# Two transformer blocks on one core: expert choices made one head earlier, and four modulation halves moved from POOL to PE

## The chip, the cores and the metric

The kernel runs on one core of one Trainium2 chip. The metric is device time in microseconds (us): the time of one execution of the whole program. Names of engines: PE is TensorE (matmuls), DVE is VectorE, ACT is ScalarE, POOL is GpSimd, SP is SyncE, which here only issues DMAs. All data are float32.

## What is computed

One sequence of 256 tokens of width 1024 goes through two blocks. Every modulation row (shift, scale, gate) is a product of one conditioning vector with a 1024-wide matrix.

```python
def first_block(x, c, ...):
    mod = (silu(c) @ w_ada + b_ada)            # shift1, scale1, gate1, shift2, scale2, gate2
    h = rmsnorm(x, norm1_w) * (1.0 + scale1) + shift1
    proj = h @ w_in
    mix = concat([hgrn2_group(proj), short_conv_group(proj)]) @ w_out
    x = x + gate1 * mix
    h = rmsnorm(x, norm2_w) * (1.0 + scale2) + shift2
    x = x + gate2 * peer(h, ...)
    return rmsnorm(x, final_norm_w)

def peer(h, w_query, sub_keys, expert_u, expert_v):   # per block of 128 tokens
    q = (xb @ w_query).reshape(T, 8, 2, 128)
    s = einsum('thpk,hpnk->thpn', q, sub_keys)          # 2 x 128 scores a head
    top_s, top_i = top_k(s, 16)
    best_s, best_pos = top_k(all 256 sums of the two halves, 16)
    idx = the 16 chosen of 16384 experts;  gate = softmax(best_s)
    act = gelu(einsum('td,thkd->thk', xb, expert_u[idx]))
    return einsum('thk,thkd->td', gate * act, expert_v[idx])

def second_block(x, c, ...):                # NSA attention, then MoBA attention
    for i in range(2):
        shift, scale, gate = split(silu(c) @ ada_w[i] + ada_b[i], 3)
        h = rms_norm(x, norm_g[i]) * (1 + scale) + shift
        x = x + gate * (nsa_mixer(h) if i == 0 else moba_mixer(h))
```

## The kernel before

**Stages.** The program first makes the modulation halves of the first block, its projections, the recurrent mixer and the convolution (`phase_a`). Then comes PEER (`phase_b`): two halves `t` of 128 tokens with eight heads `h` each, 16 heads in a list `seq`. The second block (`phase_c`) is a generator that `phase_b` steps from the ninth head on, and that ends the program.

**A head of PEER.** `query(h)` multiplies the normalized tokens with 256 columns of the query weights on PE (the matmul helper is L242) and ACT copies the result. `scores(h)` multiplies it with the subkeys (L823) and ACT copies it into a tile `sc` (for `t` = 0; two buffers). `topk(t, h)` finds the 16 experts on DVE (L836 to L883): maxima, indices, a table of sums, and at the end two tiles `ix` of row numbers and a gate `gt`. It is a generator that yields four times, so that its pieces can stand between other work. `dots(t, h, k)` gathers row `k` of `expert_u` for all 128 tokens by an indirect DMA from POOL's queue (L899, 512 KB) and multiplies and sums it with the tokens on DVE (L910). After the sixteenth, ACT applies gelu. `weigh` multiplies with the gate. `combine(t, h, k)` gathers the row of `expert_v` (L899 again), ACT makes a diagonal of weights (L935), and PE adds the weighted rows into PSUM (L937). The gathers of the first heads share eight buffers `gb`; later the sixteen `w` buffers of the weights come in.

**The order in the loop.** In head `i` of `seq`, for `k` from 0 to 15, the loop issues a dot of head `i` and, from `k` = 3 on, a combine of head `i` − 1. `pick` is `topk` of head `i` + 1, one piece of which is issued behind the dot at certain `k` (`PICK`, in the first head from `k` = 10 on), the rest behind the sixteenth dot. `query(h + 2)` is issued ahead of a head of the first half, `scores(h + 2)` at `k` = 13. Ahead of the loop a block of raised priority does `mixed(0)` (residual, norm and transposed tokens of the first half), query, scores and `topk` of head 0 for `t` = 0, `rows(0)`, `mixed(1)`, and query and scores of head 0 for `t` = 1. The row `ada15` is made behind head 1.

**Weights.** `stream` loads the weights through SP's queue in the order in which they are listed, two ahead of their use. A weight is four tiles of 512 KB from a ring of sixteen buffers `w`. A tile is loaded when the last reader of its buffer is through.

**Modulation halves.** `ada(r, w)` makes one half (512 numbers) of a row on PE: eight matmuls (L416), a copy by ACT, four transposes (L425), a reduction and an addition by DVE into `colv`. Four halves of the second block are made differently. `tick` loads a quarter of the weight into `val` from POOL's queue (L149), multiplies it there by the conditioning vector (L159) and adds it up (L160, L162). `ada_sum` then sums over partitions by four matmuls of one column (L170) and adds on DVE (L172). The four are rows 20, 21 (first needed for `norm_T(0, ...)`, the norm of the second attention), 18 and 19. `step` calls `tick` now and then in the course of the second block, `ready` completes what is left.

**The attention of the second block.** `attention` runs eight heads in a row (`k` below counts them); each has scores (L1406, mask L1213), a maximum (L1216), an exponential on ACT (L1225), the scaling by the sums (L1227, L1232), transposes (L1244) and the product with the values (L1262). The generator's user puts other work between the heads: `ada17` at `k` = 1, the gates at 2, the first half of the output projection (`out_proj`, L1314) at 4 and 5, `ada22` and the next norm at 6, `ada23` at 7.

Of the kernel before, what the change touches and what calls it, by code (L numbers as in the profile page):

```python
# [28 lines left out]
CBEATS = 3  # L29
# [40 lines left out]
class Net:  # L70
    def __init__(self, ctx, tc, d, out):
        self.tc, self.nc, self.d, self.out = tc, tc.nc, d, out
        self.ctx = ctx
        self.cp = ctx.enter_context(Pool(tc, "cp"))
        self.ps = ctx.enter_context(tc.tile_pool(name="ps", bufs=1, space=PSUM))
        self.n = 0
        self.later = []
        self.pend, self.hooks = [], []
        self.wait = False
        self.turn = 0  # L80
        self.rests, self.ahead, self.loads, self.awbuf = [], [], [], []
        self.pc = self.am = None
# [21 lines left out]
    def step(self):  # L104
        self.turn += 1
        if self.awbuf:
            self.settle(self.turn)
            self.tick()
        due = []
        for x in self.later:  # L110
            x[0] -= 1
        due = [x for x in self.later if x[0] <= 0]
        self.later = [x for x in self.later if x[0] > 0]
        for _, fn in due:
            fn()
# [25 lines left out]

    def tick(self):

        nc = self.nc
        while self.loads and len(self.ahead) < len(self.awbuf):
            r, q = self.loads.pop(0)
            w = self.awbuf.pop(0)
            self.awbuf.append(w)
            nc.gpsimd.dma_start(w, self.ada_src(r)[q * 256:q * 256 + 256].rearrange("(k p) n -> p k n", p=P))  # L149
            self.ahead.append((r, q, w))  # L150
        if not self.ahead or (self.ahead[0][1] == 0 and len(self.rests) == 2):
            return
        r, q, w = self.ahead.pop(0)
        if q == 0:
            self.n += 1
            self.adas = self.pc2.tile([P, 512], F32, name=f"adas{self.n}", tag="adas", bufs=2)
        s = self.adas
        c = (0 if r < 12 else 8) + q * 2
        nc.gpsimd.tensor_tensor(w, w, self.ca[:, c:c + 2, None].to_broadcast([P, 2, 512]), op=ALU.mult)  # L159
        nc.gpsimd.tensor_tensor(s, s if q else w[:, 1, :], w[:, 0, :], op=ALU.add)  # L160
        if q:
            nc.gpsimd.tensor_tensor(s, s, w[:, 1, :], op=ALU.add)  # L162
        if q == 3:
            self.rests.append((self.turn + CBEATS, lambda: self.ada_sum(r, s)))

    def ada_sum(self, r, s):

        p = self.bank()
        for j in range(4):
            self.nc.tensor.matmul(p[:, j:j + 1], s[:, j * P:(j + 1) * P], self.one, start=True, stop=True)  # L170
        v, hf = divmod(r, 2)
        self.nc.vector.tensor_add(self.colv[:, v, hf * 4:hf * 4 + 4], p[:, 0:4], self.bt[:, r * 4:r * 4 + 4])  # L172

    def ready(self, n):

        while len(self.loads) + len(self.ahead) > n * 4:
            self.tick()
            if len(self.rests) == 2:
                self.settle()
        self.settle()  # L180

    def settle(self, i=None):

        while self.rests and (i is None or self.rests[0][0] <= i):
            self.rests.pop(0)[1]()
# [597 lines left out]
    def phase_b(self):  # L783
# [32 lines left out]
        def scores(h, ts=(0, 2)):  # L816
            if ts[0] == 0:
                sc[0, h] = bq.tile([P, 256], F32, name=f"sc{h}", tag="sc", bufs=2)
# [152 lines left out]
        with self.tc.high_priority():  # L971
# [4 lines left out]
            self.rows(0)  # L976
            self.mixed(1)
            query(0, (1, 2))
            scores(0, (1, 2))
# [5 lines left out]
        query(1)  # L985
        scores(1)
        for i, (t, h) in enumerate(seq):
            if t == 0 and h < 6:
                query(h + 2)
            pick = topk(*seq[i + 1]) if i < 15 else iter(())  # L990
            if i == 8:
                self.rows(1)
            for k in range(16):
# [6 lines left out]
                if (k in PICK) if i else k >= 10:  # L1000
# [4 lines left out]
                if t == 0 and h < 6 and k == 13:  # L1005
                    scores(h + 2)
            go(pick)
            if i == 14:
# [9 lines left out]
            if i == 1:  # L1018
# [306 lines left out]
    def phase_c(self, pool):  # L1325
# [7 lines left out]
        def w1_(hf):  # L1333
            def part(q):
# [9 lines left out]
             wt("ks2", W, 1536, False), wt("kw2", W, 2048, False), wt("q02", W, 0, False), w1_(0), w1_(1), wt("q1", W, 512), wt("z0", W, 2608), A(16), wt("z1", W, 3120), A(17)] +  # L1344
            [wt("wo0", d["nsa_w_out_2"][0], 0, False), wt("wo1", d["nsa_w_out_2"][0], 512, False), A(22), A(23),
# [129 lines left out]
        self.awbuf = [val[0].rearrange("p k n -> p (k n)").rearrange("p (a b) -> p a b", a=2)]  # L1475
        self.loads = [(r, q) for r in (20, 21, 18, 19) for q in range(4)]
        self.tick()
# [57 lines left out]
        self.awbuf.append(val[1].rearrange("p k n -> p (k n)").rearrange("p (a b) -> p a b", a=2))  # L1535
# [60 lines left out]
        for k in self.attention([(1, i) for i in range(8)], False, score, value, weigh, zT, oT, extra):  # L1596
# [8 lines left out]
            elif k == 2:  # L1605
                self.drain()
                self.z_close(zT, oT)
                gn = self.gate_rows(8, self.bp, "gn")
            elif k == 4:
# [3 lines left out]
            elif k == 5:  # L1613
                next(op)
            elif k == 6:
                self.drain()
                self.ready(2)
# [4 lines left out]
            elif k == 7:  # L1622
                self.ada(23, get("ada23"))
                self.ready(0)
                self.awbuf = []
# [98 lines left out]
```

## Time and profile before

| | |
|---|---|
| time, median of 3 runs | 1273.39 us (1272.66 to 1278.49) |
| the profiled execution | 1271.74 us, of which the span 1270.0 us |
| PE busy in the span | 1073.0 us (84%) |
| DVE busy | 818.5 us (64%) |
| POOL busy | 580.4 us (46%) |
| ACT busy | 436.6 us (34%) |
| TensorE's granted clock, mean | 0.959 of 2.4 GHz |
| read from HBM | 394.90 MB |

The span goes from the first instruction to the last; 1.74 us of the execution lie outside it. Times in the rows below count from the start of the span. A row of an order of time gives the start, the duration, the instruction and, in brackets, how long the engine had been idle and what ended that. A group of instructions gives count, busy time, mean duration and idle time ahead of it. The DMA share is the mean share of the core's 16 DMA engines that were at work. The first gather stands at 215.72 us and the last part begins at about 945 us, when the gathers are over.

### The profile page before, as it was taken

The page shows a single profiled execution, that of the slowest core. Times are in us where ns is not written, and L with a number is a line of the kernel's source. Part 1 is how long each engine was busy: PE and PEld are TensorE (multiplying, and loading weights), DVE is VectorE, ACT ScalarE, POOL GpSimd, SP SyncE. Part 2 cuts the span into 40 slices and gives each one's busy share as a digit, 9 for nine tenths or more (in the row PEclk, how much of TensorE's full clock was granted, in tenths as well). Part 3 has the DMA queues.
Part 4 walks back from the last instruction along what each step waited for, and adds up shares of the span by engine and source line. Part 5 has one row for each costly group of instructions (what it writes and reads, how often), then busy time and mean ns, then how long its engine had stood idle before and what let it go on. Part 6 is the DMA issues. An engine that isn't in the chain of part 4 may idle for free.

```text
span 1270.0 us, 14586 instructions
## 1 busy us (share of the span) xinstructions
PE 1073.0 (84%) x4484; PEld 608.2 (48%) x4484; DVE 818.5 (64%) x2124; ACT 436.6 (34%) x939; POOL 580.4 (46%) x607
## 2 busy tenths in 40 slices
PE   6799999889877777777597777889999978798988
PEld 1789678655322222332232223334444656356866
DVE  3667555765676668756876756658735776667674
ACT  2643454212222222222342112224333443155661
POOL 0000001365777777675777766676724566500000
PEclk9899999989999999899899989999999979899989
DMA  9789876789999999998999999999999649133410
GB/s 323 272 286 327 284 243 237 292 322 328 383 417 415 415 414 415 412 415 347 365 410 409 409 406 405 406 408 398 374 398 320 200 170 343 34 133 109 157 67 34
DMA packets 144305, 396.93 MB, mean 313 GB/s; under 512 B 15246, under 2 KB 21604, under 8 KB 144228
## 3 DMA queue, kind: packets, MB, share of 16 engines
q0 software_dynamic: 76032, 276.86, 55.5%
q1 hardware_dynamic: 67852, 119.03, 26.7%
q8 instruction: 36, 0.59, 0.2%
q14 instruction: 41, 0.34, 0.1%
q10 hardware_dynamic: 344, 0.11, 0.0%
HBM read 394.90 MB, written 1.05 MB: 312 GB/s over the span
## 4 chain that ended last, share of the span: by engine, by line
PE 46%; DMA 23%; DVE 14%; issue 8%; POOL 6%; ACT 4%; SPq 0%; POOLq 0%; ACTq 0%; DVEq 0%
DMA gb<-in_peer_u_dram,ix 13%; PE peer L937 13%; DMA gb<-in_peer_v_dram,ix 7%; POOL gb L899 6%; PE pa L242 6%; PE pa L244 5%; PE pa L246 4%; PE pa L245 4%; DVE gb L910 4%; PE pa L416 2%; DMA w<-in_w_ada_dram 2%; PE po L1262 1%; DVE e L1232 1%; DVE wl L194 1%; PE pa L1244 1%
## 5 line engine op out<-in xcount | busy, mean ns | idle before, releaser
L937 PE MATMUL peer<-gb,dg 128*128 128x512 f32 x1008 | 485.4, 618 | 123.0 <-DMA gb<-in_peer_v_dram,ix 67.9
L910 DVE SCALAR_TENSOR_TENSOR gb<-gb,h 128x1024 f32<-128x1024 f32 x256 | 309.8, 1216 | 189.8 <-DMA gb<-in_peer_u_dram,ix 171.4
L937 PEld LDWEIGHTS peer<-gb,dg 128*128 128x128 f32 x1008 | 183.1, 194 | 393.0 <-issue 264.9
L899 POOL DMA_INDIRECT gb<-in_peer_u_dram,ix x256 | 241.4, 943 | 153.9 <-issue 52.5
L899 POOL DMA_INDIRECT gb<-in_peer_v_dram,ix x256 | 242.4, 947 | 108.1 <-issue 50.8
L935 ACT ACTIVATE dg<-ident,wgt 128x128 f32<-128x128 f32 x252 | 98.2, 400 | 453.0 <-PE peer L937 377.7
L194 DVE TENSOR_TENSOR wl<-w,wh 128x1024 fp32r<-128x1024 f32 x76 | 96.5, 1284 | 25.6 <-ACT wh L193 18.6
L193 ACT CAST wh<-w 128x1024 fp32r<-128x1024 f32 x76 | 77.9, 1051 | 25.5 <-DMA w<-in_nsa_w_in_dram 7.1
L790 POOL IOTA iota<- 128x54 f32 x1 | 0.2, 188 | 168.1 <-DVE wl L194 168.1
L242 PE MATMUL pa<-w,val 128*128 128x512 f32 x144 | 66.8, 606 | 0.1
L242 PE MATMUL pa<-h2T,w 128*128 128x256 f32 (+1 forms) x288 | 63.6, 371 | 0.3 <-ACT h2T L770 0.2
L242 PEld LDWEIGHTS pa<-h2T,w 128*128 128x128 f32 x288 | 52.3, 197 | 12.8 <-issue 5.8
L416 PE MATMUL pa<-w,ca 128*32 128x512 f32 x320 | 48.4, 622 | 7.2 <-ACT ca L353 4.5
L159 POOL TENSOR_TENSOR val<-val,ca 128x1024 f32<-128x1024 f32 x16 | 32.3, 2019 | 45.5 <-DMA val<-in_ada_w_dram 45.5
L244 PE MATMUL pa<-h1H,wh 128*128 128x256 f32 x160 | 45.8, 287 | 4.6 <-ACT wh L193 4.6
L245 PE MATMUL pa<-h1L,wh 128*128 128x256 f32 x160 | 45.4, 284 | 0.0
L246 PE MATMUL pa<-h1H,wl 128*128 128x256 f32 x160 | 45.2, 285 | 0.0
L242 PEld LDWEIGHTS pa<-w,val 128*128 128x128 f32 x144 | 28.0, 197 | 34.5 <-issue 32.3
L1232 DVE TENSOR_SCALAR e<-e,su 128x128 f32<-128x128 f32 (+1 forms) x96 | 37.9, 458 | 0.6
L244 PEld LDWEIGHTS pa<-h1H,wh 128*128 128x128 f32 x160 | 30.9, 193 | 5.0 <-ACT wh L193 5.0
L1225 ACT ACTIVATE e<-pb,mx 128x256 f32<-128x256 f32 x48 | 22.1, 476 | 26.5 <-DVE mx L1220 21.6
L246 PEld LDWEIGHTS pa<-h1H,wl 128*128 128x128 f32 x160 | 31.0, 195 | 0.3 <-DVE wl L194 0.3
(426 smaller groups left out, 1684.6 us busy)
## 6 DMA issues: line engine op xcount, KB each, us to landing
w<-in_w_ada_dram SPq DMA_DIRECT2D x48, 512.0 KB, 5.0
w<-in_nsa_w_in_dram SPq DMA_DIRECT2D x44, 512.0 KB, 10.9
w<-in_ada_w_dram SPq DMA_DIRECT2D x32, 512.0 KB, 6.9
w<-in_w_in_dram SPq DMA_DIRECT2D x28, 512.0 KB, 9.2
w<-in_moba_w_in_dram SPq DMA_DIRECT2D x20, 512.0 KB, 4.7
w<-in_peer_w_query_dram SPq DMA_DIRECT2D x16, 512.0 KB, 8.0
val<-in_ada_w_dram POOLq DMA_DIRECT2D x16, 512.0 KB, 5.4
w<-in_w_out_dram SPq DMA_DIRECT2D x8, 512.0 KB, 6.4
```

Of the source, the lines that this page charges most:

```text
L193: nc.scalar.copy(flat(h), flat(w))
L194: (second or nc.vector).tensor_tensor(flat(l), flat(w), flat(h).bitcast(F32), op=ALU.subtract)
L242: nc.tensor.matmul(out, lhs[0], rhs[0], start=start, stop=stop, skip_group_check=True)
L244: nc.tensor.matmul(out, lhs[0], rhs[0], start=start, stop=False, skip_group_check=True)
L245: nc.tensor.matmul(out, lhs[0], rhs[1], start=False, stop=False, skip_group_check=True)
L246: nc.tensor.matmul(out, lhs[1], rhs[0], start=False, stop=stop, skip_group_check=True)
L416: nc.tensor.matmul(p[32 * g:32 * g + 32, :], self.ca[:, co + kk:co + kk + 1].to_broadcast([P, 32]), self.wk(w, kk, 0, 512)[0], start=(k == ...
L899: nc.gpsimd.indirect_dma_start(out=b, out_offset=None, in_=table, in_offset=bass.IndirectOffsetOnAxis(ap=ix[k // 8][:, k % 8:k % 8 + 1], a ...
L910: i = v.scalar_tensor_tensor(b, b, 1.0, self.h2, op0=ALU.mult, op1=ALU.mult, accum_out=a[:, k:k + 1])
L935: nc.scalar.activation(dg, self.ident, AF.Copy, scale=w)
L937: nc.tensor.matmul(acc[t][:, n * 512:(n + 1) * 512], dg, b[:, n * 512:(n + 1) * 512], start=(h == 0 and k == 0), stop=(h == 7 and k == 15))
L1232: v.tensor_scalar(e[:, u, s], e[:, u, s], su[:, u, s:s + 1], None, op0=ALU.mult)
```

## The change

Two things are changed.

Choices. `topk` of head 1 (for `t` = 0), with the query and scores that it needs, is put ahead of the first dots, between `rows(0)` and `mixed(1)`; the second half of the tokens of query and scores follows for both heads behind `mixed(1)`. In the loop every index is one further: `query(h + 3)`, `scores(h + 3)`, and `pick` is `topk` of head `i` + 2. `sc` has three buffers. `PICK` holds for the first head too. `ada15` is made behind head 0. The pool of the choices is closed one head earlier.

Modulation. `tick`, `ada_sum`, `ready` and `settle` are gone. The four halves are made by `ada`: rows 20 and 21 at `k` = 3, rows 18 and 19 at `k` = 5. Their weights stand in the stream, 20 and 21 behind 17, 18 and 19 behind the output weights and ahead of 22 and 23.

```diff
         def scores(h, ts=(0, 2)):
             if ts[0] == 0:
-                sc[0, h] = bq.tile([P, 256], F32, name=f"sc{h}", tag="sc", bufs=2)
+                sc[0, h] = bq.tile([P, 256], F32, name=f"sc{h}", tag="sc", bufs=3)
...
             go(topk(0, 0))
             self.rows(0)
+            query(1, (0, 1))
+            scores(1, (0, 1))
+            go(topk(0, 1))
             self.mixed(1)
-            query(0, (1, 2))
-            scores(0, (1, 2))
+            for h in range(2):
+                query(h, (1, 2))
+                scores(h, (1, 2))
...
-        query(1)
-        scores(1)
+        query(2)
+        scores(2)
         for i, (t, h) in enumerate(seq):
-            if t == 0 and h < 6:
-                query(h + 2)
-            pick = topk(*seq[i + 1]) if i < 15 else iter(())
+            if t == 0 and h < 5:
+                query(h + 3)
+            pick = topk(*seq[i + 2]) if i < 14 else iter(())
...
-                if (k in PICK) if i else k >= 10:
+                if k in PICK:
...
-                if t == 0 and h < 6 and k == 13:
-                    scores(h + 2)
+                if t == 0 and h < 5 and k == 13:
+                    scores(h + 3)
             go(pick)
-            if i == 14:
+            if i == 13:
...
-            if i == 1:
+            if i == 0:
                 self.ada(15, get("ada15"))
...
-             ... A(16), wt("z1", W, 3120), A(17)] +
-            [wt("wo0", d["nsa_w_out_2"][0], 0, False), wt("wo1", d["nsa_w_out_2"][0], 512, False), A(22), A(23),
+             ... A(16), wt("z1", W, 3120), A(17), A(20), A(21)] +
+            [wt("wo0", d["nsa_w_out_2"][0], 0, False), wt("wo1", d["nsa_w_out_2"][0], 512, False), A(18), A(19), A(22), A(23),
              wt("mk", M, 1024), wt("mq0", M, 0), ...
...
-        self.awbuf = [val[0].rearrange("p k n -> p (k n)").rearrange("p (a b) -> p a b", a=2)]
-        self.loads = [(r, q) for r in (20, 21, 18, 19) for q in range(4)]
-        self.tick()
...
+            elif k == 3:
+                self.ada(20, get("ada20"))
+                self.ada(21, get("ada21"))
             elif k == 4:
                 wo = [get("wo0"), get("wo1")]
                 op = self.out_proj((oT,), wo, 0, gn)
                 next(op)
             elif k == 5:
                 next(op)
+                self.ada(18, get("ada18"))
+                self.ada(19, get("ada19"))
             elif k == 6:
                 self.drain()
-                self.ready(2)
                 self.ada(22, get("ada22"))
...
             elif k == 7:
                 self.ada(23, get("ada23"))
-                self.ready(0)
-                self.awbuf = []
```

Where it moves instructions. DVE, ahead of the first dots of PEER. `ix` and `gt` are what `topk` of head 0 ends with, `tkm<-sc` is how a choice begins, `gb<-gb,h` is a dot. Line numbers of the kernel after are 50 lower than those before here. Before:

```order
L881 RECIPROCAL tkn_2042<-tkn_2042 128x1
L871 TENSOR_TENSOR tkc_292_2023<-tkc_292_2023,tkc_2013 128x432
L882 TENSOR_SCALAR gt_2044<-gt_2044,tkn_2042 128x16
L872 TENSOR_REDUCE tkx_2024<-tkc_292_2023 128x8
L873 CAST ix_2026<-tkx_2024 128x8
L910 SCALAR_TENSOR_TENSOR gb_2169,act_2168<-gb_2169,h_2048 128x1024
```

After, the same place:

```order
L832 TENSOR_SCALAR gt_2044<-gt_2044,tkn_2042 128x16
L822 TENSOR_REDUCE tkx_2024<-tkc_292_2023 128x8
L794 MAX_INDEX tki_2082<-tkm_2081,sc_2076 128x8
L823 CAST ix_2026<-tkx_2024 128x8
L795 MATCH_REPLACE tks_2083<-tkm_2081,sc_2076 128x128
L793 MAX tkm_2081<-sc_2076 128x8
L796 MAX tkm_2081<-tks_2083 128x8
L794 MAX_INDEX tki_2082<-tkm_2081,sc_2076 128x8
L797 MAX_INDEX tki_2082<-tkm_2081,tks_2083 128x8
L795 MATCH_REPLACE tks_2089<-tkm_2081,sc_2076 128x128
L799 TENSOR_SCALAR tkm_2081<-tki_2082 128x16
L796 MAX tkm_2081<-tks_2089 128x8
```

Before, the first dot follows on the last `ix` of head 0 and the choice of head 1 begins behind the eleventh dot; after, that choice (`tkm_2081`) begins within the end of head 0's, and goes on between the first dots.

PE, where the sixth head of the attention ends and `ada22` begins. `pb<-maskb` is the mask of the next scores, `pa<-w,ca` a matmul of `ada`, `pa<-ident,os` its transposes, `pa<-ident,e` the transposes of the attention. Line numbers after are 46 to 50 lower. Before:

```order
L1213 MATMUL pb_7369<-maskb,identb 128x2x128
L170 MATMUL pa_7390<-one,adas_7088 128x1 x4
L416 MATMUL pa_7404<-w_7247,ca 32x512
L416 MATMUL pa_7404<-w_7249,ca 32x512
L416 MATMUL pa_7404<-w_7251,ca 32x512
```

After:

```order
L1167 MATMUL pb_7406<-maskb,identb 128x2x128
L375 MATMUL pa_7427<-ident,os_7380 128x128 x4
L366 MATMUL pa_7443<-w_7336,ca 32x512
L366 MATMUL pa_7443<-w_7338,ca 32x512
L366 MATMUL pa_7443<-w_7340,ca 32x512
L1198 MATMUL pa_7475<-ident,e_7311 128x128 x3
L366 MATMUL pa_7443<-w_7342,ca 32x512
```

The sum over `adas` is gone, the last of the added halves' transposes (row 19) stand in its place, and the matmuls of row 22 have transposes of the attention between them. SP's queue has sixteen loads more, and POOL's listing ends, but for two fills of `xn`, with the last gather.

## Rows read from the trace of the kernel before

**Rows 1.** Stretches: us; busy of PE, PEld, DVE, ACT, POOL; clock; DMA share; GB/s.

```profile
207.00:219.00 12.00, 11.32 (x69) 10.02 (x70) 8.43 (x44) 5.75 (x15) 2.67 (x3) 1.00 0.41 139
245.00:250.00 5.00, 3.26 (x12) 2.77 (x13) 5.00 (x15) 2.42 (x4) 0.00 (x0) 0.78 0.04 16
250.00:255.00 5.00, 5.00 (x22) 4.27 (x22) 4.93 (x28) 1.90 (x4) 0.58 (x1) 0.88 0.02 5
```

**Rows 2.** POOL in order of time around the hole: start, us, instruction [idle before <-releaser].

```profile
238.19 0.94 POOL L899 DMA_INDIRECT gb<-in_peer_u_dram,ix  x1 [0.88 <-DVE gb L910]
254.42 1.05 POOL L899 DMA_INDIRECT gb<-in_peer_u_dram,ix  x1 [15.29 <-DVE ix L873]
```

**Rows 3.** DVE in order of time: first dot, first choice row, last dot.

```profile
220.19 1.22 DVE L910 SCALAR_TENSOR_TENSOR gb<-gb,h 128x1024 f32<-128x1024 f32 x1 [3.30 <-DMA gb<-in_peer_u_dram,ix]
...
242.19 0.29 DVE L843 MAX8 tkm<-sc 128x8 f32<-128x128 f32 x1
...
249.38 1.22 DVE L910 SCALAR_TENSOR_TENSOR gb<-gb,h 128x1024 f32<-128x1024 f32 x1
```

**Rows 4.** PE in order of time, from the queries to the first combines.

```profile
208.80 4.71 PE L242 MATMUL pa<-h2T,w 128*128 128x128 f32 x32
...
214.53 7.07 PE L242 MATMUL pa<-h2T,w 128*128 128x256 f32 x32
...
240.96 1.92 PE L416 MATMUL pa<-w,ca 128*32 128x512 f32 x16
246.74 0.66 PE L425 MATMUL pa<-ident,os 128*128 128x128 f32 x4 [3.86 <-ACT os L420]
...
266.03 3.75 PE L937 MATMUL peer<-gb,dg 128*128 128x512 f32 x4 [4.27 <-DMA gb<-in_peer_v_dram,ix]
...
271.92 1.88 PE L937 MATMUL peer<-gb,dg 128*128 128x512 f32 x4
273.63 1.46 PE L242 MATMUL pa<-h2T,w 128*128 128x256 f32 x6
274.93 1.88 PE L937 MATMUL peer<-gb,dg 128*128 128x512 f32 x4
```

**Rows 5.** Groups by line, 955 to 1100 us, POOL: xcount | busy, mean ns | idle.

```profile
L159 POOL TENSOR_TENSOR val<-val,ca 128x1024 f32<-128x1024 f32 x16 | 32.3, 2019 | 45.5 <-DMA val<-in_ada_w_dram 45.5
```

**Rows 6.** Groups by line, 1030 to 1100 us, DVE.

```profile
L1232 DVE TENSOR_SCALAR e<-e,su 128x256 f32<-128x256 f32 x20 | 19.4, 1021 | 0.1
```

**Rows 7.** Groups by line, 1180 to 1250 us, DVE.

```profile
L1232 DVE TENSOR_SCALAR e<-e,su 128x256 f32<-128x256 f32 x16 | 4.5, 348 | 0.1
```

**Rows 8.** Waits of PE, 955 to 1100 us: waited for, total, times, longest.

```profile
PE po L1262 <- DVE os L1314: 8.3, 1, 8.3
PE pb L1406 <- ACT e L1225: 6.8, 1, 6.8
PE pa L1244 <- DVE e L1232: 3.3, 3, 1.5
PE pa L1174 <- DVE kd L1169: 2.4, 1, 2.4
```

**Rows 9.** DVE in order of time, the second run of scalings.

```profile
1091.37 6.01 DVE L1232 TENSOR_SCALAR e<-e,su 128x256 f32<-128x256 f32 x4
```

**Rows 10.** Stretches of the last part, columns as in rows 1.

```profile
1100.00:1110.00 10.00, 10.00 (x25) 4.43 (x24) 3.05 (x9) 1.93 (x8) 0.00 (x0) 0.77 0.00 0
1100.00:1130.00 30.00, 30.00 (x191) 16.51 (x190) 18.95 (x52) 12.88 (x35) 0.00 (x0) 0.92 0.20 71
```

**Rows 11.** PE in order of time, the same sixteen matmuls at two clocks.

```profile
1067.56 1.09 PE L1262 MATMUL po<-eT,V 128*64 128x128 f32 x16
...
1098.04 1.98 PE L1262 MATMUL po<-eT,V 128*64 128x128 f32 x16 [8.31 <-DVE os L1314]
```

**Rows 12.** SP's queue in order of time.

```profile
1055.64 7.86 SPq L129 DMA_DIRECT2D w<-in_ada_w_dram  x8
```

**Rows 13.** Issues of 1035 to 1130 us: xcount, KB, us to landing.

```profile
w<-in_ada_w_dram SPq DMA_DIRECT2D x9, 512.0 KB, 10.4
```

More of the change, by code (lines that the diff above doesn't have):

```diff
@@ L28 @@
 IDLE = 8
-CBEATS = 3
 SIDE = (1, 5, 9, 13)
@@ L80, in __init__ @@
         self.turn = 0
-        self.rests, self.ahead, self.loads, self.awbuf = [], [], [], []
         self.pc = self.am = None
@@ L105, in step @@
         self.turn += 1
-        if self.awbuf:
-            self.settle(self.turn)
-            self.tick()
         due = []
@@ L140, in half_row @@
         return self.tmp([P, 512], tag="xn" if self.am else "os")
[L142 to L185, printed above, removed]
     def split(self, w, second=None):
@@ L1343, in phase_c @@
             [wt("q1a", W, 512, False), wt("ks", W, 1536, False), wt("kw", W, 2048, False), wt("q0", W, 0, False), wt("kc", W, 1024, False),
-             wt("ks2", W, 1536, False), wt("kw2", W, 2048, False), wt("q02", W, 0, False), w1_(0), w1_(1), wt("q1", W, 512), wt("z0", W, 2608), A(16), wt("z1", W, 3120), A(17)] +
-            [wt("wo0", d["nsa_w_out_2"][0], 0, False), wt("wo1", d["nsa_w_out_2"][0], 512, False), A(22), A(23),
+             wt("ks2", W, 1536, False), wt("kw2", W, 2048, False), wt("q02", W, 0, False), w1_(0), w1_(1), wt("q1", W, 512), wt("z0", W, 2608), A(16), wt("z1", W, 3120), A(17), A(20), A(21)] +
+            [wt("wo0", d["nsa_w_out_2"][0], 0, False), wt("wo1", d["nsa_w_out_2"][0], 512, False), A(18), A(19), A(22), A(23),
              wt("mk", M, 1024), wt("mq0", M, 0), wt("mq1", M, 512), wt("mz0", M, 1536), wt("mz1", M, 2048),
@@ L1474, in phase_c @@
             self.split_T(val[0], hT, kk, 0)
-        self.awbuf = [val[0].rearrange("p k n -> p (k n)").rearrange("p (a b) -> p a b", a=2)]
-        self.loads = [(r, q) for r in (20, 21, 18, 19) for q in range(4)]
-        self.tick()
         yield
@@ L1534, in phase_c @@
             self.split_T(val[1], hT, kk, 1)
-        self.awbuf.append(val[1].rearrange("p k n -> p (k n)").rearrange("p (a b) -> p a b", a=2))
         w = get("q1")
```

## The prediction

> **What bounds the kernel now.** The page first, for PE's share of the span, the largest. It is an average over stages, so the two places of the change are read by themselves: by tables of stretches, then engine by engine in order of time.
>
> The head of PEER. The DMA engines are busy 4% and 2% of the time in the two slices from 245 to 255 us [rows 1]. That hole is POOL's: the sixteenth gather of head 0 issues at 238.19, the next starts at 254.42, after 15.29 us of waiting for `ix`, which `topk` of head 1 writes [rows 2]. DVE starts that `topk` only at 242.19, after eleven dots of head 0, and goes on with it between and behind the other five, the last of which starts at 249.38 [rows 3]. PE is then without work: the first weighting of rows of v starts at 266.03, after 4.27 us of waiting for its gather [rows 4].
>
> The last part. From 955 to 1100 us POOL multiplies and adds for the four modulation halves [rows 5]. In 1030 to 1100 DVE's 128x256 scaling at L1232 takes 1021 ns on average; in 1180 to 1250, with POOL silent, 348 [rows 6, 7]. PE waits for such a scaling, for an exponential behind slowed DVE work, for `kd`, and once 8.3 us for L1314 [rows 8], which stands on DVE behind two runs of four scalings, the second of 6.01 us [rows 9]. After such a pause TensorE's granted clock is a mixture of its two levels, 2.4 and 1.2 GHz (0.77 over ten busy us, [rows 10]), and sixteen L1262 matmuls take 1.98 us instead of 1.09 [rows 11].
>
> **The head, part by part.** `topk` of head 1 is issued ahead of the dots of head 0, and `topk` of head 2 between them. In DVE's listing the pieces of head 1 stand in front of and between the first dots, where DVE has idle time: the first dot starts at 220.19 after 3.30 us of waiting for its rows [rows 3]. So it is free from 216.9, and then has sixteen dots of 1.22 us and two choices of 8.4 (head 0's, all that DVE does in the first slice of [rows 1]): 216.9 + 19.5 + 16.8 = 253.2 without a wait. I take 254.5 for the end of head 0's last dot, instead of 250.6. Against that, head 1's rows are known by an estimated 235, and its u gathers can follow the sixteenth of head 0 as fast as dots free buffers (eight in this stage). By 254.4 I count eight gathers of it, some 10 us of transfer. The v rows of head 0 then lie ready, and the weighting waits only for gelu and `weigh`, an estimated 4.5 us behind the last dot: first combine at 259 instead of 266, a gain of 7.
>
> Two things take back from it. `query` of head 1 is made in two halves of tokens, each at 4.71 (head 0's second half) instead of 7.07 at once [rows 4], 2.3 us of PE, which has room there. And more of the queries is left when combining begins: from 271.92 on a v gather's matmuls (1.71 us) alternate with six query matmuls (1.30) [rows 4], 3.0 us where POOL's issue of a u and a v gather would take 2.5 (two of 0.94 and 0.31). About 5 us more of queries, at a loss of 0.5 for each 1.30, is 2 us. **Head: 7 − 2 = 5 us.** Bounds: 0, if the pace behind the hole is PE's anyway; 10, the hole's two slices in full (4.8 + 4.9). I take 5, as the wait of 15.29 is the row nearest and PE's alternation keeps it from being had in full.
>
> Behind it, up to the last heads, the gathers, dots and matmuls are the same, but for choices that stand one head earlier: nothing, and the gain passes on. `ada` of row 15 moved from the second to the first head, the third `sc` buffer and three memsets moved on POOL lie under the gathers; without that cover they are 1.92 + 0.66 us of PE [rows 4] at most.
>
> **The last part.** Removed on POOL: 16 multiplications (2.0 us each, [rows 5]), 28 additions, 16 loads. DVE gets its undisturbed times. Of PE's waits [rows 8] the 8.3 goes in full: eight scalings at 1021 − 348 ns are 5.4, the second run alone gives 4.6, the small operations between them are slowed too, and what is left of DVE's work lies under PE's own. The 3.3 goes. Of the 6.8 I take 2, of `kd` 2: the work ahead of them is slowed in part only. That is 15.6. Clock: 0.77 over ten busy us is 2.3 us lost [rows 10], and about as much after the two other long pauses; with one of these left, 5. **Relief 20**, next late is PE itself.
>
> Added on PE: four halves of 1.92 and 0.66 [rows 4], 10.3, less four sums of four short matmuls, 0.5 each by the transposes' row: **8 us**, all on PE's path. Their four ACT copies and DVE reductions lie under it. The 16 loads of 512 KB go from POOL's queue to SP's, the bytes are the same.
>
> New waits. Each weight is four buffers of a ring of sixteen that SP's queue fills in order. Rows 18 and 19 are loaded when PE has used 20 and 21; 22 and 23 when it has used 18 and 19; moba's k when it has used 22. Before, 22 and 23 were issued from 1055.64, in 7.86 us [rows 12], long before use. Now 22 must come between the fifth and the sixth head of the attention: four issues of about 1 us and their transfer, an estimated 7 us, about as long as one head. PE takes its instructions in order, so a late load holds the heads behind it. I take 2 us for all of it; bounds 0 and 12 (the median landing of 10.4, [rows 13], and 2 of low clock). **Last part: 20 − 8 − 2 = 10 us**, bounds 0 and 17.
>
> **Sum.** 5 + 10 = 15 off the profiled execution of 1271.74, which lies 1.65 below the runs' median of 1273.39: **1258** by the median. Bounds 0 and 27 off, 1246 to 1273.
>
> One row speaks against the head: next to DVE's choice the gather at 254.42 took 1.05 us, against 0.94 at 238.19 [rows 2]. At 0.11 more, sixteen gathers lose 1.8 us, which they have. The Trainium skill, "SBUF — State Buffer", section "SBUF: two separate sides", says more: while DVE runs an operation that takes both ports, POOL is locked out of the pair that they share and cannot write the descriptors of its own DMAs. By that rule gathers would stand still for a choice; that is rival 4.
>
> **Rivals.**
> 1. The head gains nothing. Either the pace behind the hole is PE's, 3.0 us for a pair of gathers [rows 4], and what comes earlier waits for queries; or the change doesn't do what it says, since eight buffers, freed by dots that now stand behind two choices, hold head 1's gathers as `ix` did. Against it: PE idles 4.27 before the first combine. Only the last part counts: 1273.4 − 10 = 1263. Chance 0.17.
> 2. POOL's relief is not PE's: DVE and ACT set the pace of the attention's heads, and the halves are pure addition. Against it: from 1100 on, with POOL silent, PE is busy 30.00 of 30 us [rows 10]. Relief 10 − 8 − 2, head 3: 1270. Chance 0.17.
> 3. Slower, by the ring: each of the loads of 18, 19, 22 and 23 is waited for on PE with its whole landing time (10.4, [rows 13]) and 2 of low clock. That is 4 × 12 = 48 in place of the 2: 1304. It decides from 24 us of such waits on, two of the four, where the time passes 1279.8. Against it: a pair issues together, so that the second is hidden by the first. Chance 0.09.
> 4. POOL is held by DVE's choices: head 1's gathers come later by one choice (8.4) than forecast, head −3 instead of +5: 1266. The 1.05 against 0.94 speaks against it. Chance 0.07.
>
> **How the numbers follow.** Forecast 0.50, 1258, own range 1250 to 1266. A measurement of this kernel can tell about 0.5% (6.4 us) from no change: faster ends at 1267.0, slower starts at 1279.8. Faster: 0.48 of the forecast, 0.15 of rival 1, 0.05 of rival 2, 0.04 of rival 4: 0.72. Same: 0.02, 0.02, 0.11, 0.03 and 0.01 of rival 3: 0.19. Slower: 0.08 of rival 3 and 0.01 of rival 2: 0.09. The range goes from 1245, the best case of the sum, to 1272, past rival 2.
>
> **What would show it.** Right: DMA engines busy over 0.7 of 245 to 255, no wait of POOL for `ix` over 5 us, the first combine near 259; L1232 near 350 ns throughout, no 8.3 us wait on PE. Wrong: PE waiting at L416 for `w` loads by over 2 us at rows 18 or 22 (rival 3); gathers above 1.1 us beside the choices (rival 4); the first combine early but pairs of gathers 3 us apart for longer than before (rival 1); PE still waiting for DVE in the attention's heads without POOL (rival 2).

## The result and the profile after

The kernel after takes 1249.61 us (median of 6 runs, 1246.89 to 1253.74), the kernel before 1273.62 (6 runs beside it). The ratio is 0.983, 95% interval 0.980 to 0.986: faster by 24 us in the medians, by 18 to 25 us by the interval. Its profiled execution takes 1246.89 us, the shortest of the six. The page of the kernel after, part 1 and the chain of work that ended last, and that chain before:

```profile
PE 1077.0 (86%) x4564; PEld 610.7 (49%) x4564; DVE 783.0 (63%) x2128; ACT 438.9 (35%) x944; POOL 494.2 (40%) x547
...
PE 59%; DMA 19%; DVE 7%; issue 6%; POOL 4%; ACT 4%; ACTq 0%; POOLq 0%; DVEq 0%
```

```profile
PE 46%; DMA 23%; DVE 14%; issue 8%; POOL 6%; ACT 4%; SPq 0%; POOLq 0%; ACTq 0%; DVEq 0%
```

POOL has 86 us less, DVE 36 us less although it has four instructions more, PE 4 us more. PE's share of the chain has grown from 46% to 59%, at the cost of DVE's and DMA's. To say where the time went I cut both traces at three marks: the start of the first gather, the first combine on PE, and the end of the last combine.

| us | before | after | difference |
|---|---|---|---|
| start to first gather | 215.7 | 213.3 | −2.4 |
| first gather to first combine | 50.3 | 43.7 | −6.6 |
| first gather to last combine (PEER) | 732.8 | 724.9 | −7.9 |
| last combine to the end | 321.5 | 306.9 | −14.6 |
| span | 1270.0 | 1245.1 | −24.9 |

The first line is no part of the change: other traces of both kernels start gathering between 215 and 218 us. The marks in the rows, before (L937) and after (L887): the last combines, from a window that begins at 925 us:

```profile
924.72 23.77 PE L937 MATMUL peer<-gb,dg 128*128 128x512 f32 x55
```

```profile
924.69 13.47 PE L887 MATMUL peer<-gb,dg 128*128 128x512 f32 x31
```

The head of PEER. Stretches after, columns as in [rows 1], where the slices from 245 to 255 had a DMA share of 0.04 and 0.02:

```profile
240.00:245.00 5.00, 5.00 (x24) 4.19 (x23) 5.00 (x21) 0.00 (x0) 1.89 (x3) 1.00 1.03 419
245.00:250.00 5.00, 3.56 (x29) 1.78 (x29) 4.65 (x21) 2.25 (x7) 2.80 (x3) 1.00 1.02 409
250.00:255.00 5.00, 5.00 (x26) 4.43 (x25) 5.00 (x15) 1.37 (x2) 1.06 (x1) 1.00 0.54 193
255.00:260.00 5.00, 5.00 (x18) 3.08 (x17) 5.00 (x20) 1.98 (x5) 3.64 (x4) 1.00 0.82 272
```

The hole is filled but for half a slice. POOL after, in order of time: the first gather of head 1, and the two longest waits among its gathers, which stand where 15.29 us stood [rows 2]:

```profile
236.01 0.94 POOL L849 DMA_INDIRECT gb<-in_peer_u_dram,ix  x1 [0.31 <-issue]
...
242.34 0.94 POOL L849 DMA_INDIRECT gb<-in_peer_u_dram,ix  x1 [4.15 <-DVE tki L797]
...
252.68 1.06 POOL L849 DMA_INDIRECT gb<-in_peer_u_dram,ix  x1 [3.89 <-DVE gb L860]
```

Head 1's gathers follow head 0's without a pause. What they wait for then is a free buffer, that is DVE, which has the pieces of a choice between the dots that free them. The row at 242.34 names a tile of the choice (`tki`), but it starts 0.27 us behind the end of head 0's eleventh dot (242.07), as that at 252.68 starts 0.28 behind the end of the sixteenth.

The last part. DVE's scaling (L1232 before, L1186 after) in 1000 to 1080 us, and PE's waits from 940 to 1080 us (waited for, total, times, longest). In [rows 6] and [rows 8] there stood 1021 ns and waits of 8.3, 6.8, 3.3 and 2.4:

```profile
L1186 DVE TENSOR_SCALAR e<-e,su 128x256 f32<-128x256 f32 x24 | 7.1, 349 | 0.2
```

```profile
PE pa L1525 <- DVE xn L1515: 2.4, 1, 2.4
PE pb L1360 <- ACT e L1179: 1.8, 1, 1.8
PE pa L1128 <- ACT os L1077: 0.8, 1, 0.8
```

Of these the 2.4 for `xn` is new: before, PE waited 0.2 us for it.

The halves that PE now makes (L366 and their transposes), in order of time:

```profile
1052.04 3.64 PE L366 MATMUL pa<-w,ca 128*32 128x512 f32 x32
1055.61 0.66 PE L375 MATMUL pa<-ident,os 128*128 128x128 f32 x4
...
1066.72 0.60 PE L375 MATMUL pa<-ident,os 128*128 128x128 f32 x4
...
1077.82 3.64 PE L366 MATMUL pa<-w,ca 128*32 128x512 f32 x32
...
1086.15 1.10 PE L366 MATMUL pa<-w,ca 128*32 128x512 f32 x6
```

The rows at 1052.04 and 1077.82 are rows 20, 21 and 18, 19, that at 1086.15 is the begin of row 22. None has idle time ahead of it: none of these matmuls waited for its weights. SP's queue after issued the loads of rows 18, 19, 22 and 23 in one stretch of 29.79 us instead of 7.86 [rows 12]:

```profile
1053.97 29.79 SPq L124 DMA_DIRECT2D w<-in_ada_w_dram  x16
```

### The profile page after: what moved, and what is told of

It is laid out like the page before. It is cut to its first block, busy times and chain, and to the rows that moved or that the text cites. A ratio compares the mean times of both kernels' runs of the same rounds, so it can differ in the third digit from the quotient of the medians.

```text
span 1245.1 us, 14741 instructions
## 1 busy us (share of the span) xinstructions
PE 1077.0 (86%) x4564; PEld 610.7 (49%) x4564; DVE 783.0 (63%) x2128; ACT 438.9 (35%) x944; POOL 494.2 (40%) x547
## 4 chain that ended last, share of the span: by engine, by line
PE 59%; DMA 19%; DVE 7%; issue 6%; POOL 4%; ACT 4%; ACTq 0%; POOLq 0%; DVEq 0%
PE peer L887 17%; PE pa L192 10%; DMA gb<-in_peer_v_dram,ix 9%; DMA gb<-in_peer_u_dram,ix 9%; PE pa L194 5%; PE pa L196 5%; PE pa L195 5%; POOL gb L849 4%; PE pa L366 3%; DVE gb L860 3%; PE po L1216 2%; PE pa L1198 1%; ACT dg L885 1%; PE pa L522 1%; PE pb L1360 1%
## 5 line engine op out<-in xcount | busy, mean ns | idle before, releaser
L887 PE MATMUL peer<-gb,dg 128*128 128x512 f32 x1008 | 486.7, 621 | 110.8 <-DMA gb<-in_peer_v_dram,ix 67.9
L887 PEld LDWEIGHTS peer<-gb,dg 128*128 128x128 f32 x1008 | 185.0, 195 | 380.2 <-issue 273.3
L144 DVE TENSOR_TENSOR wl<-w,wh 128x1024 fp32r<-128x1024 f32 x76 | 91.5, 1220 | 19.7 <-ACT wh L143 14.2
L366 PE MATMUL pa<-w,ca 128*32 128x512 f32 x384 | 57.4, 625 | 7.0 <-ACT ca L303 4.6
L377 DVE TENSOR_REDUCE adac<-pa 128x4 f32<-128x16 f32 x24 | 4.1, 171 | 48.1 <-PE pa L375 47.9
L195 PEld LDWEIGHTS pa<-h1L,wh 128*128 128x128 f32 x160 | 31.2, 195 | 0.0
```

Source lines behind the costliest of these rows:

```text
L144: (second or nc.vector).tensor_tensor(flat(l), flat(w), flat(h).bitcast(F32), op=ALU.subtract)
L195: nc.tensor.matmul(out, lhs[0], rhs[1], start=False, stop=False, skip_group_check=True)
L366: nc.tensor.matmul(p[32 * g:32 * g + 32, :], self.ca[:, co + kk:co + kk + 1].to_broadcast([P, 32]), self.wk(w, kk, 0, 512)[0], start=(k == ...
L887: nc.tensor.matmul(acc[t][:, n * 512:(n + 1) * 512], dg, b[:, n * 512:(n + 1) * 512], start=(h == 0 and k == 0), stop=(h == 7 and k == 15))
```

## The experiments

In the tables below PEER is first gather to last combine, and the rest is last combine to the end. The chip of the first pair of traces is not on record. The first four runs below share one chip; where a later run was on another this is said. The measure is always the kernel before, timed beside it on the same chip.

### Each part alone

The choices alone, on the kernel before. The edit is the choice part of the diff, of which two pieces are shown, with the modulation left on POOL:

```diff
             self.rows(0)
+            query(1, (0, 1))
+            scores(1, (0, 1))
+            go(topk(0, 1))
             self.mixed(1)
...
-            pick = topk(*seq[i + 1]) if i < 15 else iter(())
+            pick = topk(*seq[i + 2]) if i < 14 else iter(())
```

> The kernel before with the choices alone made earlier; the four modulation halves stay on POOL. Theory (the two parts add): the part of the span between the first gather and the last combine shortened by 7.9 us in the trace after, and nothing of that hangs on the halves: 8 us below before, ratio 0.994 (0.992 to 0.996). The first combine comes 6 to 7 us nearer to the first gather. Rival (the head gains nothing, the last part alone counts): the hole in the DMA is filled, but the last combine ends where it did, ratio 0.998 to 1.002.

Measured: 1266.53 us (10 runs), ratio 0.994 (0.989 to 0.998). In the trace PEER takes 723.1 us, the rest 322.0.

The halves alone, on the kernel after, with the choice part put back (two pieces shown):

```diff
-            query(1, (0, 1))
-            scores(1, (0, 1))
-            go(topk(0, 1))
             self.mixed(1)
...
-            pick = topk(*seq[i + 2]) if i < 14 else iter(())
+            pick = topk(*seq[i + 1]) if i < 15 else iter(())
```

> The kernel after with the choices as before; only the halves are moved to PE. Theory: from the last combine on, the trace after is 14.6 to 16 us shorter, so 15 us below before, ratio 0.988 (0.985 to 0.991); with the run of the choices alone the two gains sum to that of the whole change. Rival (the relief of DVE is mostly not on PE's path, and the whole change gains in PEER): ratio above 0.993.

Measured: 1258.91 us (4 runs), ratio 0.987 (0.982 to 0.992). PEER 731.7, the rest 307.9. So the parts add: one works in PEER and leaves the rest alone, the other the other way round, and 0.994 times 0.987 is 0.981. The rival of the second run is out by its interval; that of the first, which the interval touches at 0.998, by the trace, where the last combine ends 9.7 us earlier. A wait of PE for a weight stands in this trace, in PE's waits from 940 to 1110 us; the traces of four later runs have one too, of 0.3 to 1.0 us, those of the kernel after none:

```profile
PE pa L366 <- DMA w<-in_ada_w_dram: 0.8, 1, 0.8
```

### What in the last part was slow: POOL's arithmetic

```diff
-        nc.gpsimd.tensor_tensor(w, w, self.ca[:, c:c + 2, None].to_broadcast([P, 2, 512]), op=ALU.mult)
-        nc.gpsimd.tensor_tensor(s, s if q else w[:, 1, :], w[:, 0, :], op=ALU.add)
-        if q:
-            nc.gpsimd.tensor_tensor(s, s, w[:, 1, :], op=ALU.add)
+        nc.gpsimd.tensor_tensor(s[:, 0:4] if q else s, w[:, 0, 0:4] if q else w[:, 0, :],
+                                self.ca[:, c:c + 1].to_broadcast([P, 4 if q else 512]), op=ALU.mult)
+        nc.gpsimd.tensor_tensor(s[:, 0:4], s[:, 0:4], w[:, 1, 0:4], op=ALU.add)
```

> The kernel before with POOL's arithmetic on the four halves cut down: the 16 multiplications work on 4 columns of 1024 (the first of each half on 512), the additions on 4; the loads on POOL's queue, the sums on PE and all waits between them stay, so the four modulation halves are not what they should be. Theory (DVE and POOL hold each other up in the last part): L1232 falls from 1021 to about 350 ns, PE's waits of 8.3 and 3.3 us go, and as no work is added on PE the gain is larger than by the halves on PE, 20 to 23 us below before, ratio 0.982 to 0.985. Rival (the loads on POOL's queue, the sums or the places where the kernel waits for the halves cost the time): ratio 0.995 to 1.0, L1232 still above 700 ns.

Measured: 1251.51 us (4 runs), ratio 0.982 (0.977 to 0.987). PEER 732.7 as before, the rest 302.0. DVE's scaling (L1230 in this kernel) in 1000 to 1080 us, and PE's waits from 940 to 1110:

```profile
L1230 DVE TENSOR_SCALAR e<-e,su 128x256 f32<-128x256 f32 x20 | 5.8, 344 | 0.1
```

```profile
PE pb L1404 <- ACT e L1223: 4.8, 1, 4.8
PE pa L1172 <- DVE kd L1167: 1.0, 1, 1.0
PE cmp L1545 <- DVE kcT L1526: 0.9, 1, 0.9
PE pa L1573 <- DVE xn L1563: 0.2, 1, 0.2
```

The sixteen loads still go through POOL's queue, the sums and all waits between them are there, and POOL still runs 32 operations, 28 of them of 0.31 to 0.34 us, four of 1.2. The other long ones are gone, and with them the 1021 ns, the 8.3 and the 3.3 us [rows 6, 8]. So it is the long operations of POOL that held DVE up, and not its loads or the places at which the kernel waits for the halves. Two rows of the kernel before, DVE and POOL in order of time, show how:

```profile
1090.25 1.08 DVE L1415 TENSOR_TENSOR su<-su,gate 128x4 f32<-128x4 f32 x1
```

```profile
1090.06 1.26 POOL L160 TENSOR_TENSOR adas<-adas,val 128x512 f32<-128x512 f32 x1
```

DVE's operation, which takes 0.15 us on average in the trace after (L1369), starts within POOL's and ends with it, at 1091.33 and 1091.32. The Trainium skill, "SBUF — State Buffer", section "SBUF: two separate sides", has this as an exclusive lock on a port pair that the two engines share, held for a whole instruction. These two rows fit that; a test of the ports themselves is not among the runs. The rest is 19.5 us shorter than before: that is the relief without a price. The halves on PE, at 307.9, cost 5.9 us of it.

### One choice ahead or two

The choice of head 1 stays ahead of the first dots, but in the loop the choice is one head ahead, as before; nothing is chosen during head 0.

```diff
-        query(2)
-        scores(2)
         for i, (t, h) in enumerate(seq):
-            if t == 0 and h < 5:
-                query(h + 3)
-            pick = topk(*seq[i + 2]) if i < 14 else iter(())
+            if t == 0 and h < 6:
+                query(h + 2)
+            pick = topk(*seq[i + 1]) if 0 < i < 15 else iter(())
...
```

> The kernel after, but in the loop the choice is one head ahead, as before: only head 1 is chosen ahead of the first dots, and during head 0 nothing is chosen. Theory (the hole is that head 1's choice comes late, no more): the hole stays filled, DVE has one choice of 8.4 us less among head 0's dots, so head 0's last dot and the first combine come up to 5 us earlier than after: 1244 to 1250, ratio 0.977 to 0.982. Rival (two heads ahead are needed, else the hole comes one head later): 1255 to 1258, ratio 0.986 to 0.989, with POOL waiting for ix by 5 us or more at the begin of head 2's gathers.

Measured: 1248.28 us (4 runs), ratio 0.980 (0.975 to 0.984). PEER 720.5, the rest 307.6. Stretches of this kernel, columns as in [rows 1]:

```profile
245.00:250.00 5.00, 5.00 (x25) 4.40 (x24) 4.91 (x12) 0.54 (x2) 3.57 (x5) 1.00 1.03 418
250.00:255.00 5.00, 4.27 (x24) 3.56 (x23) 4.97 (x17) 2.02 (x6) 3.21 (x4) 1.00 1.03 419
```

The hole is filled without a remainder. Two heads ahead are not needed: no later hole appears, and the trace of PEER is 4 us shorter than that of the kernel after. The two intervals overlap, so that as a time this lead is not shown.

### Does PE's query work take the gain back?

A table of when the gathers of u of a head begin, in us from the first gather, read from POOL in order of time (head 8 is the first of the second half of tokens):

| first gather of u of head | 1 | 2 | 3 | 5 | 8 | 15 | last combine ends |
|---|---|---|---|---|---|---|---|
| before | 38.7 | 87.0 | 131.7 | 212.2 | 334.2 | 651.3 | 732.8 |
| after | 22.7 | 75.3 | 122.4 | 203.0 | 326.0 | 641.2 | 724.9 |
| after, third trace | 22.2 | 73.2 | 120.4 | 201.2 | 323.8 | 639.1 | 724.2 |
| head 1 only | 22.7 | 74.4 | 122.5 | 202.1 | 325.0 | 641.0 | 720.5 |
| half query (below), again | 22.9 | 74.6 | 114.4 | 194.5 | 317.7 | 632.5 | 719.0 |

Two rows of the kernel after from which such numbers come, head 0's first gather and head 3's:

```profile
213.29 1.25 POOL L849 DMA_INDIRECT gb<-in_peer_u_dram,ix  x1 [40.92 <-ACT h2T L720]
...
335.71 0.94 POOL L849 DMA_INDIRECT gb<-in_peer_u_dram,ix  x1 [0.30 <-issue]
```

Head 1 begins 16.0 us earlier than before, head 2 11.7, head 3 9.3, and from there on it stays at 8 to 10. To see whether PE's queries eat the 7 us, half of the query matmuls of heads 3 to 7 was left out:

```diff
+                kd = KD // 2 if h > 2 else KD
-                for k in range(KD):
+                for k in range(kd):
...
```

> The kernel after, with half of the query matmuls of heads 3 to 7 left out (four of eight blocks of the inner dimension), so that the choices of these heads are others; 5 times 3.5 us of PE's work is gone. Theory (behind the hole PE's queries between the combines set the pace, 3.0 us for a pair of gathers instead of 2.5): 5 to 10 us below the kernel after, ratio 0.973 to 0.979. Rival (the gathers' bytes set it): within 1.5 us of the kernel after, ratio 0.980 to 0.985.

Measured: 1330.19 us (10 runs), ratio 0.994 (0.990 to 0.999). The kernel after, run beside it on the same chip, had the same:

> The kernel after, unchanged, as the measure for the three that run beside it: 1247 to 1252 us, ratio 0.980 to 0.985.

Measured: 1330.49 us (12 runs, 1321 to 1338), ratio 0.996 (0.992 to 0.999). Both were on another chip, on which the kernel before takes 1339.47. The trace after has there 808.4 us of PEER and 308.1 of the rest: the gathers are slow, 365 GB/s from 400 to 600 us, against 399 in the third trace after. Stretches of the two, columns as in [rows 1], the slow chip first:

```profile
400.00:600.00 200.00, 133.86 (x252) 52.81 (x250) 108.61 (x308) 33.97 (x79) 130.95 (x139) 0.82 0.96 365
```

```profile
400.00:600.00 200.00, 149.75 (x311) 55.81 (x309) 133.72 (x372) 52.38 (x117) 145.26 (x170) 0.95 1.00 399
```

On that chip the question could not be decided, and the gain is less than half. So the kernels were run once more beside the kernel before and the kernel after:

> The kernel before, unchanged, for a trace beside the three others. From first gather to last combine 733 us and 321 to 323 us behind it where the gathers run as fast as in its first trace; where they run as slowly as in the four runs ahead of this one (792 to 808 us from first gather to last combine), over 800 us, and the part behind the last combine still 321 to 323: that part hangs on no gather.

Measured: 1275.31 us (a single run), PEER 732.5, the rest 322.9, on a third chip, with gathers as fast as in the first traces.

> The kernel after, unchanged, as the measure for the two below. Behind the last combine 306 to 309 us, 14 below before wherever it runs. From first gather to last combine 8 us below before if the gathers run as in the first traces (ratio 0.980 to 0.985); where they are slow, one theory (the hole of the DMA is filled, so its bytes are won at any pace) says 8 us again, ratio 0.982 to 0.985, the other (at the slower pace other waits take the gain) 0 to 3, ratio 0.987 to 0.990.

Measured: 1251.76 us (6 runs), ratio 0.984 (0.980 to 0.987), PEER 724.2, the rest 308.1: 8.3 and 14.8 us less than the kernel before beside it, as in the first pair of traces.

> The kernel after with half of the query matmuls of heads 3 to 7 left out, run again (the choices of these heads are others). Theory as it stands by the traces so far (PEER follows the first combine; PE's queries between the combines take nothing back): first gather to last combine within 2.5 us of the kernel after, ratio within 0.002 of its. Rival (PE's queries set the pace up to 325 us): 5 to 10 us shorter.

Measured: 1245.71 us (6 runs), ratio 0.978 (0.974 to 0.982), PEER 719.0. My theory at that moment, that PE takes nothing back, fell: the time is 6 us below that of the kernel after. Stretches of the kernel after (third trace) and, below it, with half the queries:

```profile
280.00:300.00 20.00, 19.32 (x64) 11.45 (x64) 9.27 (x19) 4.82 (x11) 11.77 (x13) 1.00 0.95 353
300.00:320.00 20.00, 18.65 (x72) 12.38 (x71) 13.89 (x47) 4.28 (x11) 12.40 (x14) 1.00 0.94 336
```

```profile
280.00:300.00 20.00, 19.40 (x65) 9.94 (x64) 8.63 (x16) 5.91 (x12) 14.04 (x15) 1.00 1.02 406
300.00:320.00 20.00, 15.04 (x29) 5.38 (x29) 18.27 (x60) 6.13 (x15) 14.99 (x16) 0.91 1.03 418
```

With the queries whole, PE is busy 19 of 20 us and the DMA engines move 336 to 353 GB/s; with half of them the rate is 406 to 418, and from 300 us on PE has room (15.04 of 20). The table has all of it in head 2, 47.2 us long in the third trace after and 39.8 here. The rows that are gathered in that time are those of heads 1 and 2, whose choices this edit leaves as they are. PE's queries do set the pace from about 290 to 320 us. How much of the lead they take is counted below.

### A version with fewer queries in the way

PE stands still for 4.5 us in the kernel after before the first combine: the scores of head 0's second half wait for a copy on ACT, which stands behind the exponential of head 1's gate, and that waits for DVE. PE, then ACT, in order of time:

```profile
225.73 1.22 PE L773 MATMUL pa<-skT,qT 128*128 128x128 f32 x4 [4.51 <-ACT qT L762]
```

```profile
225.03 0.31 ACT L830 ACTIVATE gt<-tkb,tkn 128x16 f32<-128x16 f32 x1 [6.97 <-DVE tkb L816]
```

So the query of head 1 was made whole, behind `mixed(1)`, once with the loop two heads ahead and once with it one head ahead, as in the run of head 1 only:

```diff
-            query(1, (0, 1))
-            scores(1, (0, 1))
-            go(topk(0, 1))
             self.mixed(1)
-            for h in range(2):
-                query(h, (1, 2))
-                scores(h, (1, 2))
+            query(0, (1, 2))
+            scores(0, (1, 2))
+            query(1)
+            scores(1)
+            go(topk(0, 1))
```

> The kernel after, with the query of head 1 made whole, behind mixed(1), and the choice of head 1 issued behind it; the choices of the loop stay two heads ahead. In the trace after PE stands still for 4.5 us at 225.7, since the copy of a query waits on ACT behind the exponential of head 1's gate, and the query in two halves costs 2.3 us more of PE. Theory (from 200 to 325 us PE's work sets the pace): both come off, 3 to 6 us below the kernel after, ratio 0.977 to 0.981. Rival (DVE's two choices among the dots of head 0 set the pace, PE has room): within 1 us of the kernel after, or up to 3 us above, as head 1's choice starts later.

Measured, on the slow chip: 1327.08 us (12 runs), ratio 0.994 (0.989 to 0.998), against 0.996 of the kernel after: no difference that the runs can tell.

> As the one before, and in the loop the choice is one head ahead, so that only head 1 is chosen early. Theory (PE's pace): no better than with the choices two ahead, since the queries up to 325 us are the same, 3 to 6 us below the kernel after, ratio 0.976 to 0.981. Rival (DVE's choices among the dots): the first combine comes earlier than with two choices, 5 to 8 us below the kernel after, ratio 0.974 to 0.978.

Measured, on the slow chip: 1318.41 us (6 runs), ratio 0.987 (0.981 to 0.992), where the kernel after has 0.996 (0.992 to 0.999).

> Whole query and choice of head 1 behind mixed(1), the loop's choice one head ahead, run again beside the kernel after. Theory (what the first combine gains on the first gather is gained in full): first combine 40 to 42 us behind the first gather instead of 43.7, and first gather to last combine 3 to 5 us shorter than after, ratio 0.975 to 0.980. Rival (its lead over the kernel after in the runs ahead of this one was the spread of slow gathers): within 1.5 us of the kernel after.

Measured, on the third chip: 1251.19 us (6 runs), ratio 0.983 (0.979 to 0.987), against 0.984 of the kernel after beside it. PEER is 3.6 us shorter in its trace (720.6), the rest 2.8 us longer (310.9). That is the rival's result: the lead of the slow chip is not there. Whether it is real on the slow chip was not tried again. So no version is shown to beat the kernel after; the two with one choice ahead have a PEER shorter by 3.6 to 4.4 us in their traces. They gain it in the last head. There, after, a v gather waits for a combine on PE:

```profile
886.47 0.94 POOL L849 DMA_INDIRECT gb<-in_peer_v_dram,ix  x1 [3.93 <-PE peer L887]
```

From the first gather of head 15 to the last combine it takes 81.5 us before, 83.7 and 85.1 after, 79.5 with the choice one head ahead. With two heads ahead no choice is left on DVE in the last two heads, and the work of the second block comes in another order among the combines; which of its instructions makes the 4 us was not tried.

## Why the prediction came out as it did

The forecast was 1258, the range 1245 to 1272; the time is 1249.6. The sign and the two mechanisms were right, the sum was 8 to 9 us too small: by the traces 4.6 us of it lie in the last part and 2.9 in the head.

**The head** was put at 7 − 2 = 5 and measured 7.9, 8.3 and, alone, 9.7 us. Head 0's last dot ends at 252.4 in the trace after, 39.1 us behind the first gather (38.8 were forecast), and the first combine stands 43.7 behind it (43.3); by the first gather it came 6.6 to 8.9 us sooner, where 7 was taken. That working holds, and so does the term of −2 for PE's queries; what was mis-sized is the 7 from which it was taken. It is the lead of the first combine, and the gathers get further ahead than that. Their lead over the first trace before, in us, counted by the gathers of u and v together as POOL issues them (16 is head 1's first):

| gather | 16 | 24 | 40 | 56 | 72 |
|---|---|---|---|---|---|
| after | 16.0 | 7.0 | 11.8 | 12.1 | 9.3 |
| after, third trace | 16.5 | 9.0 | 14.1 | 14.2 | 11.3 |
| head 1 only | 16.0 | 14.7 | 12.6 | 12.6 | 9.5 |
| half query, again | 15.8 | 7.4 | 11.4 | 15.3 | 17.3 |

The 16 us shrink to 7 within eight gathers, in the waits for buffers shown above; the run with head 1 only, which chooses nothing during head 0, keeps 14.7 there. That isn't what is missing at the end, since from gather 40 on the two are alike: up to there 5 us come back. Before, PE starts its combines later and at a lower clock, 0.66 in the ten us from 262, and 1.00 in the ten from 253 after; the first four matmuls take 3.75 us where later ones take 1.88 [rows 4]. What each of the two gives was not separated. From gather 56 to 72 it takes 22.0 us before, 24.8 in both traces after and 20.0 with half the queries, and POOL waits there for combines on PE, after:

```profile
307.59 0.93 POOL L849 DMA_INDIRECT gb<-in_peer_v_dram,ix  x1 [1.96 <-PE peer L887]
```

These 2.8 us are the term of −2. So it is 12 − 3 = 9 and not 7 − 2 = 5, and from then on the lead stays at 8 to 10.

**The last part** was put at 20 − 8 − 2 = 10 and measured 14.6 and 14.8. The relief of 20 holds as a sum: the run with POOL's arithmetic cut down has 19.5. There the waits went as the steps said: 8.3 and 3.3 gone, 2.0 of the 6.8, 1.4 of the 2.4 for `kd`, where 2 was taken. That the sum came out is in part luck: in that run PE's idle time behind the last combine falls by 17.2 us (35.6 to 18.4), where the waits were put at 15.6, and its busy time by 2.3 (285.9 to 283.6), where the clock was put at 5. Two terms on the other side were too large. The added work on PE was 8 and is 5.9: a pair of halves takes about 4.5 us by the rows above (3.57 from start to start for its matmuls, 0.4 to 0.5 for each of its transposes), 9 in all, not 10.3; and the sums that go were put at 0.5 each, without a row of theirs. A whole sum takes 0.95 us in the trace before (L170, at 1007.76). Nine less four of 0.95 is 5.2, and with the wait of 0.8 for a weight in that trace 6.0. The new waits on the ring were 2 and are 0 in the kernel after, at most 1.0 in the other traces. From the first matmul of row 18 to that of row 22 it is 8.3 us (1077.82 to 1086.15), a little more than the 7 us that were estimated for the load, and the load was there.

**The rivals.** Rival 1 (the head gains nothing) is out by the choices alone, though both its mechanisms are there: PE's pace takes 3 us, and buffers that hold the gathers take 9, of which 5 come back. Rival 2 (the relief is not PE's) is out: PE's waits for DVE in the attention's heads went. Rival 3 (the ring) is out by the rows. Rival 4, gathers held by the choices: beside choices most gathers take 0.93 or 0.94 us, but single ones take up to 1.37, over the 1.1 that was named as its sign. There are such ones before too: 13 of 512 over 1.1 us, against 16 after. All 512 take 484.6 us before and 486.8 after, so what they cost is some 2 us spread over PEER and not 8.4 in the head. The rule of the Trainium skill, "SBUF — State Buffer", section "SBUF: two separate sides", that POOL cannot write descriptors while DVE holds the pair, is hardly seen with the operations of a choice; which of them hold it was not tried. With POOL's own arithmetic the lock is seen the other way round: there DVE waited.

**What stays open.** On the slow chip the kernel after gains 0.4% only (0.992 to 0.999). The part behind the last combine is as short there as elsewhere (308.1), so what is missing is missing in PEER. An estimate from the medians: 1339.5 − 1330.5 is 9.0 us, and if the last part gives its 14.6 there too, the choices lose 5 to 6 us on that chip instead of gaining 8. The kernel before has no trace there, so this is not shown, and which wait takes it is not known.

## What to carry to other kernels

A wait that a trace shows as one long hole is worth what the stream behind it gets ahead, not what the next consumer gains: follow the starts of the transfers from one round to the next until the lead stays constant, and look at which engine eats the difference. An operation that is moved off a busy engine onto POOL is not free while DVE works in SBUF: here 32 us of multiplications and 44 us of additions cost DVE a factor of three on its scalings and the program 20 us, and the same result on PE costs 6. Where a term of a sum has no row, as the sums on PE here, look for one in the whole trace before putting it at a bound.

## What the hardware showed that I had not expected

Gathers of the same rows run at 365 GB/s on one chip and at 399 in two traces elsewhere, so that the same kernel takes 1330 or 1250 us. What is not PEER takes the same time in the three traces of the kernel after: 213 to 217 us ahead of it and 307 to 308 behind it. And after the same pause of PE, late in the second attention, a wait of 2.0 us for a scaling, the granted clock in the ten us behind it was 0.76 in the first trace before, 0.58 in the second trace of that same kernel, and 0.60 after. Ten busy us at 0.60 instead of 0.76 are 1.6 us less of work at full clock. So the same code gets a different clock from one execution to another, which may be part of the spread of 7 us among the runs of one kernel; that was not followed run by run. The rows, first and second trace before, then after, columns as in [rows 1]:

```profile
1226.00:1236.00 10.00, 9.96 (x50) 5.57 (x52) 8.56 (x25) 4.69 (x13) 0.00 (x0) 0.76 0.00 0
```

```profile
1227.98:1237.98 10.00, 10.00 (x37) 5.17 (x37) 7.61 (x22) 4.19 (x12) 0.00 (x0) 0.58 0.00 0
```

```profile
1200.00:1210.00 10.00, 10.00 (x40) 5.12 (x40) 7.56 (x21) 3.75 (x12) 0.00 (x0) 0.60 0.01 2
```
